# Twenty-nine matmuls that nobody reads, at the start of a planned two-layer transformer kernel

## The chip, the cores and the metric

The kernel runs on one core of a Trainium2 chip. A core has five engines with queues of their own: TensorE (PE, with its weight loads shown as PEld), VectorE (DVE), ScalarE (ACT), GpSimd (POOL) and SyncE (SP, which here only issues DMA transfers). Each engine works through its queue in order; semaphores hold an instruction until what it reads or overwrites is ready. The metric is the device time of one execution in microseconds (us). The kernel before takes 1548.72 us, the median of three runs (1548.48 to 1550.03).

## The reference

Two layers over 512 latent tokens and 256 context tokens of width 1024. What matters here is the opening of layer 0: a modulation vector from the conditioning, an RMS norm of the tokens, and the product with the QKV weights.

```python
silu_c = jax.nn.silu(c)
...
mod_lat = (silu_c @ ada_w[i] + ada_b[i])[:, None, :]
...
u_lat = modulate(rms_norm(h_lat, g_mix[i]), sh1, sc1)
u_ctx = modulate(rms_norm(h_ctx, g_mix[i]), csh1, csc1)
if i % N_MIXERS == 0:
    w = na_wqkv[j]
    ql, kl, vl = jnp.split((u_lat @ w).reshape(B, L, 3, H, dh), 3, axis=2)
    ...
    y_lat = neighborhood_attention(ql, kl, vl, kc, vc, na_rpb[j]) @ na_wo[j]
...
h_lat = h_lat + ga1 * y_lat
h_lat = h_lat + ga2 * squared_relu_mlp(
    modulate(rms_norm(h_lat, g_mlp[i]), sh2, sc2), mlp_w1[i], mlp_w2[i])
```

Attention adds a relative position bias to the scores (layer 0); layer 1 has sliding-window attention.

## The kernel before

The kernel holds its tokens transposed: feature tile f (0 to 7) has 128 features on the partitions and the tokens along the row. Every large product is made of three matmuls on values that are split into a high and a low part (`split`: ACT casts the high part, DVE or POOL subtracts it to get the low one).

The order of the work is not that of the source. `_build` records every operation as a step of a plan. `Plan.add` finds what each step depends on (also that a tile is read before it is overwritten), and `Plan.search` then sets the order on all engines. It goes through the program in pieces, ended by `mark()`, and for each tries many orders: a rank per step starts as the step's number, is changed by `hurry` where PE would stand still, and is shaken by random amounts that are drawn for groups of consecutive step numbers. The best order by its own table of costs is kept. Some operations have two possible engines (`gv`, `sv`, `squared`), and the search chooses between them. `build` issues all steps in that order at line 548, which is why nearly every row of the profile has this line.

The opening runs so:

- SP loads the constants (`cst`), the tokens (`xT`, four loads), and by the list `LOADS` the modulation weights of tile f (two halves `w01s[f, 0]` and `w01s[f, 1]`, by `load01`), the QKV weights of head pair 0 (`load0`), and the context tokens. `load` keeps these loads in their written order. Behind them come the QKV weights of pair 1 and the 32 transfers of `bias_tables`, which lay out the position bias in memory (`bias_i`, `bias_e`).
- `stats` squares each latent tile (ACT or DVE, four buffers) and sums it over the partitions with a matmul on the constant tile `ones`, into PSUM bank 4. ACT then makes the inverse root of it (two operations).
- `ada01(f)` makes the modulation sums of tile f: two groups of eight matmuls that are 32 columns wide, one per half of the weights. `mods01(f)` copies the sums to `row`, which is the first 128 columns of the second half's tile `w01s[f, 1]`, turns them with one small matmul on `pair`, and adds the bias on DVE. `mod0` then modulates tile f (DVE, ACT, DVE).
- `qkv0(0)` makes the QKV products of head pair 0 for six token tiles in banks 2 to 7, feature tile by feature tile as they come. A tile that is done goes through a head norm (ACT, DVE, POOL) and is transposed. `attn0(0)` follows: scores, and on DVE the position bias is added, which needs the bias loaded back from `bias_i` and `bias_e`. Products of pair 1 (256 columns) are put between.

Later pairs end in `attn0` with a multiplication by the inverse row sums, which DVE writes out and SP reads back through memory (`inv_d`), so that every partition has them.

Of the kernel before, what the change touches and what calls it, by code (L numbers as in the profile page):

```python
# [525 lines left out]
def build(nc, tc, a):  # L526

    with ExitStack() as es:
        plan, regions, cuts = _build(nc, tc, a, es)
        tiles, now, open_ = {}, -1, ExitStack()  # L530

        def real(x):
            return x.made(tiles) if isinstance(x, Late) else x

        def turn(k):

            open_.close()
            for j, (dtype, n) in enumerate(regions[k]):
                pool = open_.enter_context(tc.tile_pool(name=f"top{k}{j}", bufs=1))
                tiles[k, j] = pool.tile([128, n], dtype, name=f"R{k}{j}", tag="R")  # L540

        for step in plan.search(ROUNDS, TRIES, cuts):
            while step.epoch is not None and now < step.epoch:
                now += 1
                turn(now)
            for f, args, kw in step.calls:
                e = getattr(nc, NAMES[step.eng])
                tc.keep_in_program_order(getattr(e, f)(*map(real, args), **{k: real(x) for k, x in kw.items()}))  # L548
        open_.close()
# [16 lines left out]
def _build(nc, tc, a, es):  # L566
# [29 lines left out]
    @contextmanager  # L596
    def together():

        group.append(Step("PE"))
        yield  # L600
        plan.add(group.pop())

    v, s, g, pe, sy = (Engine(n) for n in ("vector", "scalar", "gpsimd", "tensor", "sync"))
# [3 lines left out]
    def squared(out, x):  # L607
        y = Step("ACT")
        y.forms = {"ACT": ("activation", (out, x, AF.Square), {}), "DVE": ("tensor_tensor", (), dict(out=out, in0=x, in1=x, op=ALU.mult))}
        y.calls, y.reads, y.writes = [y.forms["ACT"]], [x], [out]  # L610
        plan.add(y)
# [5 lines left out]
    def const(name, shape):  # L617
        return pool.tile(shape, F32, name=name, tag=name)
# [20 lines left out]
    banks = [psum.tile([128, 512], F32, name=f"pq{i}", tag=f"pq{i}")[:] for i in range(8)]  # L639

    class Banks:
# [3 lines left out]
        def next(self):  # L645
            self.i += 1
            return self.b[(self.i - 1) % len(self.b)]
# [14 lines left out]
    ones = const("ones", [128, 128])  # L662
# [38 lines left out]
    def load(out, in_):  # L701

        x = sy.dma_start(out, in_)
        if strict[0]:
            if strict[1:]:
                x.after = strict.pop().i
                x.deps.add(x.after)
            strict.append(x)
# [281 lines left out]
    def load0(p, units, eng=None):  # L990
        n = cols0(p)
        for q in units:
            r = (raw0 if p == 0 else raw).next(2 * n)
            load(r, a[f"wqkv0{min(p, 2)}"][max(0, p - 2), :, q * 2 * n : (q + 1) * 2 * n])
            u = (w00, w01, w0)[min(p, 2)].next()
            split(u[:, 0 : 2 * n], u[:, 2 * n : 4 * n], r, eng)
            for i in range(2):
                W0[p, 2 * q + i] = (u[:, i * n : (i + 1) * n], u[:, (2 + i) * n : (3 + i) * n])
# [388 lines left out]
    rows01, w01s = {}, {}  # L1387

    def load01(f):

        for i in range(2):
            w01s[f, i] = ada_ring.next()
            load(w01s[f, i], a["ada01"][f, :, 1024 * i : 1024 * i + 1024])

    def ada01(f):

        ps = banks[f % 2]
        for i in range(2):
            w = w01s[f, i].rearrange("p (k e n) -> p k e n", k=4, e=2)
            with together():  # L1400
                for k in range(0, 4, 2):
                    for e in range(2):
                        for j in range(2):
                            c = 32 * (2 * e + j)
                            pe.matmul(ps[c : c + 32, 0:128], s32[:, 4 * i + k + j, :], w[:, k + j, e], start=(4 * i + k == 0), stop=(4 * i + k == KT - 2), tile_position=(0, c))
        rows01[f] = w[:, 0, 0]
# [15 lines left out]
    def stats(h, R, sq, ps, summed):  # L1422

        st = Stats(R, R.shape[1], sq, ps)
        for f in range(KT):
            if not summed:
                st.step(h(f))
                continue
            q = sq.next()
            squared(q, h(f))  # L1430
            pe.matmul(ps[:, 0 : st.n], ones[:], q, start=f == 0, stop=f == KT - 1)
        st.finish(summed=summed)
# [8 lines left out]
    def more(n):  # L1441
        for _ in range(n):
            x = next(loads, None)
            if x is None:
                return
            if x == "c":
                load(hT_ctx, a["cT"])
            elif x == "w":
                load0(0, (w00.i,), g)
            else:  # L1450
                load01(x)

    more(5)
    stats(lambda f: hT_lat[:, f], Rb[:, 0:512], Ring(RX, 2048, 512, 4), banks[4], True)
    ada01(0)
    qk = qkv0(0)
    for f in range(KT):
        mods01(f)
# [33 lines left out]
    for p in range(7):  # L1492
        p_mm = Banks(2, 3, 4, 4, 4, 4) if p == 0 else Banks(4)
        at = (attn0(p), 14)
        if p < 4:
            n = (1, 3, 3, 3)[p]
# [609 lines left out]
    for gr in range(4):  # L2106
        seq = []
        n = 0
# [125 lines left out]
```

## Time and profile before

The profile is of one execution; times in it are counted from the span's start.

| | |
|---|---|
| that execution's own time | 1549.73 us |
| its span, first to last instruction | 1547.8 us |
| median of three runs | 1548.72 us |
| mean granted TensorE clock | 0.996 |
| TensorE busy | 1522.6 us |
| chain that ended last: share of PE, DVE, ACT | 92%, 4%, 2% |
| DMA, mean rate over the span | 119 GB/s |

An engine's busy time counts an instruction from start to end; on TensorE instructions overlap, and a multi-pass product of 32-bit values counts each pass. In a row of the time line stand the start, the length, the engine, the line, the operation, output and inputs, the count of merged instructions, and in brackets the idle time before with what ended it. The granted clock is the share of full speed that the TensorE clock was given.

### The profile page before, as it was taken

The numbers are of one execution on the slowest core, as the hardware profiler recorded it, in microseconds if no ns is written. First come the engines' busy times: TensorE is split into PE (matmuls) and PEld (weight loads), VectorE is DVE, ScalarE is ACT, GpSimd is POOL, SyncE is SP. The second block draws the span as 40 slices with busy tenths as digits, with TensorE's granted clock in tenths as the row PEclk, the third lists the DMA queues.
The fourth block names the chain that finished last, engine by engine and source line by source line (L and its number), as shares of the span: only waits on it lengthen the run. The fifth ranks groups of instructions, "written<-read, shape, count | busy, mean of one in ns | idle before, by whom it ended". The sixth has DMA issues, their size and how long they took to land.

```text
span 1547.8 us, 26105 instructions
## 1 busy us (share of the span) xinstructions
PE 1522.6 (98%) x9541; PEld 1350.7 (87%) x9541; DVE 1242.3 (80%) x2672; ACT 852.7 (55%) x1989; POOL 231.5 (15%) x223
## 2 busy tenths in 40 slices
PE   7999999999999999999999999999999999999999
PEld 4879888898899999999999998788778989898897
DVE  4888889867589998988888777899876897777764
ACT  4676666677466443344433454677784755555551
POOL 1110000101111322101111010321101312111110
PEclk9999999999999999999999999999999999999999
DMA  9654443215425433444444332001145343323321
GB/s 360 158 180 127 136 165 101 75 38 168 151 89 163 130 119 120 137 140 146 150 150 132 101 109 83 21 30 48 35 147 180 100 133 103 101 83 109 96 69 68
DMA packets 81473, 183.86 MB, mean 119 GB/s; under 512 B 9105, under 2 KB 26049, under 8 KB 81345
## 3 DMA queue, kind: packets, MB, share of 16 engines
q1 hardware_dynamic: 81344, 182.21, 37.0%
q8 instruction: 74, 1.21, 0.3%
q14 instruction: 55, 0.44, 0.1%
HBM read 172.64 MB, written 12.68 MB: 120 GB/s over the span
## 4 chain that ended last, share of the span: by engine, by line
PE 92%; DVE 4%; ACT 2%; DMA 1%; issue 1%; SPq 0%; POOL 0%; DVEq 0%; ACTq 0%; POOLq 0%
PE pq L548 92%; DVE FA L548 2%; DVE RA L548 1%; ACT FA L548 1%; DVE R L548 1%; ACT RA L548 0%; DMA R<-inv_d 0%; DMA FA<-bias_e 0%; DVE smalls L548 0%; ACT R L548 0%; DMA FA<-in_xT_dram 0%; SPq L548 0%; ACT smalls L548 0%; DVE mods L548 0%; POOL FA L548 0%
## 5 line engine op out<-in xcount | busy, mean ns | idle before, releaser
L548 PE MATMUL pq<-RA 128*128 128x256 f32 (+2 forms) x5906 | 1069.7, 335 | 7.8 <-DVE RA L548 4.5
L548 PEld LDWEIGHTS pq<-RA 128*128 128x128 f32 x5906 | 919.5, 190 | 95.4 <-issue 6.2
L548 PE MATMUL pq<-RA,R 128*128 128x256 f32 (+2 forms) x1896 | 339.3, 331 | 1.3 <-DVE FA L548 1.3
L548 ACT CAST RA<-FA 128x512 fp32r<-128x512 f32 (+4 forms) x390 | 232.3, 618 | 166.8 <-PE pq L548 123.3
L548 PEld LDWEIGHTS pq<-RA,R 128*128 128x128 f32 x1896 | 299.2, 189 | 26.1 <-DVE FA L548 2.1
L548 DVE TENSOR_TENSOR RA<-FA,RA 128x512 fp32r<-128x512 f32 (+4 forms) x350 | 256.0, 751 | 35.3 <-ACT RA L548 31.5
L548 DVE SCALAR_TENSOR_TENSOR FA<-pq,mods,FA 128x512 f32<-128x512 f32 (+1 forms) x323 | 201.1, 639 | 94.6 <-PE pq L548 92.6
L548 ACT ACTIVATE FA<-FA 128x256 f32<-128x256 f32 (+2 forms) x216 | 102.9, 484 | 60.0 <-DVE FA L548 48.4
L548 ACT CAST R<-FA 128x512 fp32r<-128x512 f32 x107 | 65.1, 619 | 106.0 <-PE pq L548 94.2
L548 PE MATMUL pq<-ident,FA 128*128 128x128 f32 x772 | 118.8, 275 | 4.4 <-issue 3.8
L548 POOL TENSOR_TENSOR RA<-FA,RA 128x512 fp32r<-128x512 f32 (+3 forms) x40 | 58.8, 1473 | 380.2 <-ACT RA L548 328.7
L548 ACT ACTIVATE FA<-FA,smalls 128x512 f32<-128x512 f32 (+1 forms) x120 | 88.7, 740 | 33.3 <-DVE smalls L548 32.5
L548 PEld LDWEIGHTS pq<-ident,FA 128*128 128x128 f32 x772 | 92.1, 141 | 16.6 <-issue 7.2
L548 DVE TENSOR_TENSOR FA<-FA 128x512 f32<-128x512 f32 (+3 forms) x163 | 88.7, 557 | 9.7 <-ACT FA L548 5.1
L548 ACT COPY R<-pq 128x512 f32<-128x512 f32 (+4 forms) x166 | 74.0, 469 | 34.8 <-PE pq L548 33.9
L548 ACT COPY FA<-pq 128x256 f32<-128x256 f32 (+5 forms) x114 | 44.3, 389 | 85.6 <-PE pq L548 82.7
L548 POOL TENSOR_TENSOR FA<-FA,smalls 128x256 f32<-128x256 f32 (+2 forms) x55 | 37.5, 681 | 294.5 <-DVE smalls L548 232.5
L548 DVE TENSOR_TENSOR R<-FA,R 128x512 fp32r<-128x512 f32 (+1 forms) x101 | 74.3, 743 | 8.6 <-ACT R L548 7.4
L548 ACT CAST RA<-R 128x256 fp32r<-128x256 f32 (+2 forms) x107 | 51.4, 489 | 51.2 <-PE pq L548 46.5
L548 DVE CUSTOM_DVE_ANT_0 R<-R,cst 128x512 bf16<-128x512 f32 (+1 forms) x64 | 78.5, 1226 | 0.1
L548 POOL TENSOR_TENSOR FA<-FA 128x256 f32<-128x256 f32 (+2 forms) x50 | 48.1, 970 | 188.0 <-ACT FA L548 85.9
L548 PE MATMUL pq<-R 128*64 128x256 f32 (+3 forms) x432 | 67.2, 450 | 0.7 <-DVE FA L548 0.7
(107 smaller groups left out, 1161.4 us busy)
## 6 DMA issues: line engine op xcount, KB each, us to landing
FA<-in_w_dram SPq DMA_DIRECT2D x128, 256.0 KB
FA<-in_w_dram SPq DMA_DIRECT2D x64, 512.0 KB
R<-in_ada_dram SPq DMA_DIRECT2D x54, 512.0 KB
FA<-in_ada_dram SPq DMA_DIRECT2D x26, 512.0 KB
FA<-in_wqkv_dram SPq DMA_DIRECT2D x24, 384.0 KB
FA<-in_ada_w_dram SPq DMA_DIRECT2D x16, 512.0 KB
FA<-in_wo_dram SPq DMA_DIRECT2D x16, 512.0 KB
FA<-in_wq_dram SPq DMA_DIRECT2D x8, 512.0 KB
```

The costliest lines, as they stand in the source:

```text
L548: tc.keep_in_program_order(getattr(e, f)(*map(real, args), **{k: real(x) for k, x in kw.items()}))
```

## The change

A helper `busy(n, x)` issues n matmuls of the constant tile `ones` with the first 128 columns of x, into bank 7, whose content nobody reads before the QKV products start it anew. Twenty-one of them, with `ones` as x, are written ahead of the norm sums; eight, with the second half of tile 0's modulation weights as x, behind the sums of tile 0.

```diff
+    def busy(n, x):
+        for _ in range(n):
+            pe.matmul(banks[7][:, 0:128], ones[:], x[:, 0:128], start=True, stop=True)
+
     more(5)
+    busy(21, ones)
     stats(lambda f: hT_lat[:, f], Rb[:, 0:512], Ring(RX, 2048, 512, 4), banks[4], True)
     ada01(0)
+    busy(8, w01s[0, 1])
     qk = qkv0(0)
```

The steps get other numbers, so the search draws other orders for the whole program. TensorE's queue opened so before (pq_66 to pq_73 are the PSUM banks 0 to 7, `s_82` is the silu of the conditioning, R the squares or the weights, FA and RA the large tiles):

```order
L548 MATMUL pq_70<-R_132,ones 128x512 x8
L548 MATMUL pq_66<-FA,s_82 32x128 x16
L548 MATMUL pq_67<-FA,s_82 32x128 x8
L548 MATMUL pq_66<-pair,FA 128x4
L548 MATMUL pq_67<-FA,s_82 32x128 x8
L548 MATMUL pq_66<-FA,s_82 32x128 x8
L548 MATMUL pq_68<-RA 128x512 x3
L548 MATMUL pq_69<-RA 128x512 x3
L548 MATMUL pq_70<-RA 128x512 x3
L548 MATMUL pq_71<-RA 128x512 x3
L548 MATMUL pq_67<-pair,FA 128x4
```

The same place in the changed kernel:

```order
L548 MATMUL pq_73<-ones 128x128 x21
L548 MATMUL pq_70<-R_143,ones 128x512 x7
L548 MATMUL pq_66<-FA,s_82 32x128 x8
L548 MATMUL pq_70<-R_143,ones 128x512
L548 MATMUL pq_66<-FA,s_82 32x128 x8
L548 MATMUL pq_73<-FA,ones 128x128 x8
L548 MATMUL pq_67<-FA,s_82 32x128 x8
L548 MATMUL pq_66<-pair,FA 128x4
L548 MATMUL pq_67<-FA,s_82 32x128 x8
L548 MATMUL pq_67<-pair,FA 128x4
L548 MATMUL pq_66<-FA,s_82 32x128 x8
L548 MATMUL pq_69<-RA 128x512
```

The 21 stand first, the 8 directly behind the modulation sums of tile 0, one group of those sums has moved ahead of the last norm sum, and the small product of tile 1 (`pq_67<-pair`) now stands ahead of the first QKV product and not behind twelve of them.

Further on in TensorE's queue, about the third and fourth feature tile, before:

```order
L548 MATMUL pq_71<-RA 128x512
L548 MATMUL pq_67<-R_132,s_82 32x128 x16
L548 MATMUL pq_68<-RA 128x512
L548 MATMUL pq_69<-RA 128x512
L548 MATMUL pq_70<-RA 128x512
L548 MATMUL pq_72<-FA,ones 128x256
L548 MATMUL pq_71<-RA 128x512
L548 MATMUL pq_67<-pair,R_132 128x4
L548 MATMUL pq_66<-R_132,s_82 32x128 x8
L548 MATMUL pq_66<-FA,s_82 32x128 x8
L548 MATMUL pq_67<-FA,s_82 32x128 x8
L548 MATMUL pq_66<-pair,FA 128x4
```

The same tiles now:

```order
L548 MATMUL pq_71<-RA 128x512
L548 MATMUL pq_67<-R_143,s_82 32x128 x8
L548 MATMUL pq_69<-RA 128x512
L548 MATMUL pq_67<-R_143,s_82 32x128 x8
L548 MATMUL pq_70<-RA 128x512
L548 MATMUL pq_68<-RA 128x512
L548 MATMUL pq_67<-pair,R_143 128x4
L548 MATMUL pq_68<-RA 128x512
L548 MATMUL pq_66<-R_143,s_82 32x128 x8
L548 MATMUL pq_72<-FA,ones 128x256
L548 MATMUL pq_69<-RA 128x512
L548 MATMUL pq_66<-FA,s_82 32x128 x8
```

The groups of modulation sums, which stood together, lie singly among the QKV products. From the first QKV product to the last `pair` product there were 4 visits to such groups, and there are 11 now. The last `pair` product of the opening stands behind 67 QKV products where it stood behind 93, and the first token tile has all its products after 99 of the 144 instead of 117. Over the whole program TensorE goes from products to transposes 252 times where it went 188 times.

SP's queue behind the bias tables, before (the last two table transfers, then the weights of pair 2 `wqkv02`, modulation weights `ada_w` and `ada0`, and the bias loaded back):

```order
L548 DMA bias_i_88<-in_rpb_i_dram 16x8x256
L548 DMA bias_e_89<-in_rpb_dram 16x8x128
L548 DMA FA_64<-in_wqkv02_dram 128x768 x2
L548 DMA FA_64<-in_ada_w_dram 128x1024 x2
L548 DMA FA_64<-in_ada0_dram 128x1024
L548 DMA FA_64<-bias_i_88 128x256 x2
L548 DMA FA_64<-bias_e_89 64x128 x4
```

Ahead of the tables and at their start, now:

```order
L548 DMA FA_64<-in_wqkv01_dram 128x512
L548 DMA FA_64<-in_ada_w_dram 128x1024
L548 DMA FA_64<-in_wqkv01_dram 128x512
L548 DMA bias_i_88<-in_rpb_i_dram 16x8x256
L548 DMA bias_e_89<-in_rpb_dram 16x8x128
L548 DMA FA_64<-in_wqkv01_dram 128x512
L548 DMA FA_64<-in_ada_w_dram 128x1024
L548 DMA FA_64<-in_ada0_dram 128x1024
L548 DMA FA_64<-in_wqkv01_dram 128x512
L548 DMA bias_i_88<-in_rpb_i_dram 16x8x256
```

The first two `ada_w` loads and the first `ada0` load, which stood between the tables and the bias loads, now stand ahead of 30 of the 32 table transfers; they write into the rows of the tokens that are modulated last. Behind the tables follow the two `wqkv02` loads and at once the bias. Ahead of the first score that needs the bias, TensorE's queue now has 14 more products of pair 1.

## The prediction

> **What bounds the kernel now.** I read the head of the page first, then the busy time of each engine by stretch, then the chain that ended last, then single rows of the time line.
>
> ```profile
> span 1547.8 us, 26105 instructions
> PE 1522.6 (98%) x9541; PEld 1350.7 (87%) x9541; DVE 1242.3 (80%) x2672; ACT 852.7 (55%) x1989; POOL 231.5 (15%) x223
> 0.00:5.70 5.70, 0.00 (x0) 0.00 (x0) 2.80 (x17) 2.13 (x3) 0.70 (x6) 1.00 0.64 197
> ...
> 15.30:17.50 2.20, 1.65 (x48) 1.11 (x48) 0.00 (x0) 2.13 (x3) 0.00 (x0) 1.00 1.04 425
> 17.50:20.90 3.40, 1.76 (x35) 1.24 (x36) 2.39 (x5) 1.15 (x4) 0.00 (x0) 1.00 1.07 364
> 20.90:24.30 3.40, 3.40 (x9) 2.39 (x10) 0.57 (x1) 0.77 (x3) 0.00 (x0) 0.50 1.04 402
> 24.30:27.50 3.20, 2.17 (x26) 1.62 (x24) 1.66 (x7) 1.31 (x4) 0.74 (x1) 0.99 1.03 408
> ...
> 76.40:82.60 6.20, 3.30 (x28) 1.66 (x27) 5.34 (x15) 3.63 (x12) 0.61 (x1) 0.98 0.84 259
> 82.60:86.00 3.40, 3.38 (x13) 2.91 (x14) 2.31 (x10) 2.80 (x7) 0.61 (x1) 0.53 0.97 370
> 86.00:980.00 894.00, 889.29 (x5349) 804.65 (x5348) 741.67 (x1548) 476.93 (x1108) 127.56 (x111) 1.00 0.39 123
> 980.00:987.00 7.00, 3.17 (x17) 2.43 (x16) 6.65 (x15) 1.77 (x6) 3.12 (x4) 0.99 0.13 37
> ```
>
> A row of the stretches gives its length, then busy time and instructions of PE, weight loads, DVE, ACT and POOL, the granted clock, and DMA share and GB/s. TensorE is the bound: 25.2 us of the span are without a matmul, and what PE loses it loses for good. The losses sit in few places: 5.70 at the start, 0.55 + 1.64 + 1.03 from 15.3 to 27.5, 2.90 ahead of the first attention scores, 4.71 in the 894 us behind, 3.83 at the layer boundary. Two of these stretches run at a granted clock of about 0.5, and ahead of each PE was busy only about half the time (1.76 of 3.40, 3.30 of 6.20).
>
> ```profile
> 15.34 0.70 ACT FA L548
> ...
> 16.59 1.04 ACT RA L548
> ...
> 20.74 4.78 PE pq L548 x14
> ...
> 76.29 5.31 DMA FA<-bias_e
> ```
>
> The chain has two serial pieces that this change touches. From the end of the norm sums (15.3) to the first real product (20.74) it goes through ACT and DVE. Ahead of 82 it goes through a bias load that SP's queue issues late.
>
> **The change part by part.** *Ahead: 21 matmuls.* Each is two passes of 128 columns. No row shows the form.
>
> ```profile
> 0.84 0.17 DVE L548 MEMSET ones<- 128x128 f32 x1 [0.84 <-PEq L2224]
> ...
> 6.72 0.34 PEld L548 LDWEIGHTS pq<-R,ones 128*128 128x128 f32 x1 [0.52 <-issue]
> ...
> 7.57 0.34 PEld L548 LDWEIGHTS pq<-R,ones 128*128 128x128 f32 x1 [0.52 <-issue]
> ...
> 11.47 0.63 ACT L548 ACTIVATE R<-FA 128x512 f32<-128x512 f32 x1 [1.30 <-DMA FA<-in_xT_dram]
> ...
> 13.42 0.19 PEld L548 LDWEIGHTS pq<-R,ones 128*128 128x128 f32 x1 [0.24 <-issue]
> 13.85 0.19 PEld L548 LDWEIGHTS pq<-R,ones 128*128 128x128 f32 x1 [0.24 <-issue]
> ...
> 16.05 0.63 ACT L548 ACTIVATE FA<-FA 128x512 f32<-128x512 f32 x1
> ...
> 215.06 1.36 PE L548 MATMUL pq<-ident,FA 128*128 128x128 f32 x11
> 216.18 5.35 PE L548 MATMUL pq<-RA 128*128 128x256 f32 x30
> ```
>
> A pass of the sums (same weights, 512 columns) starts every 0.85 us early and every 0.43 later: the array is at half speed at first, which the clock column does not show there. A quarter of the columns makes 0.21 and 0.11; eleven transposes of 128 columns, 0.10 each (215.06 to 216.18), say that the weight load hides. So 42 passes take 42 x 0.11 = 4.6 us at full and 42 x 0.21 = 8.8 at half speed; were each weight load of 0.34 exposed, 14.3. I take a mix, 3 us slow (14 passes) and 28 x 0.11, 6 us. They start when `ones` is there (1.0), end at about 7 (5.6 to 15.3 by the bounds), and delay the sums, whose first operand is there at 5.7. The sums cannot end before the last squares anyway, at 12.1 (row 11.47), since these wait for the last load. PE is then at full speed and has caught up: two operands (4 x 0.43) and the 32-wide group that now stands between them (0.46, below) are left, so the last pass ends at about 14.4, not 15.3: **-0.9 us**, which the chain passes on to the first product (19.8). At the upper bound it would be +7 at that point.
>
> *Behind: 8 matmuls.* 16 x 0.11 = 1.8 us (3.4 at half speed). They read the columns that ACT then overwrites with its copy of the modulation sums, so that copy waits for them. Their cover: between the last sum and that copy stand ACT's 0.70, the cast of 1.04 (both in the chain) and 0.63 (row 16.05), 2.37 us. Cost **0**; without the cover 1.8.
>
> *What they hold up: the clock.* The 17.5:20.9 stretch was at 1.76 of 3.40, and the next at 0.50. The 8 lie mostly ahead of it (14.9 to 16.7) and fill what stands there; what fills the stretch itself is the first products, from 19.8 instead of 20.74: 1.76 + 0.9 = 2.7 of 3.4. The half-speed stretch then goes: 3.40 x 0.5 = **-1.7**. (The other end is 0.) [...]
>
> *The new order.* The order is planned anew with 29 more steps, and every engine's queue differs. Three things in it I can price. First, the pair product of tile 1 now stands ahead of the products (the 1.03 us gap in 24.3:27.5 goes), but that of tile 2 comes after four to six products and waits for ACT's second modulated tile, some 0.7: **-0.3**. Second, 11 visits to the 32-wide groups lie among the products where there were 4.
>
> ```profile
> 27.49 4.83 PE L548 MATMUL pq<-RA 128*128 128x512 f32 x20 [0.65 <-ACT RA L548]
> ...
> 50.31 0.64 PE L548 MATMUL pq<-FA,s 128*32 128x128 f32 x16
> 50.77 1.06 PE L548 MATMUL pq<-R,s 128*32 128x128 f32 x32
> 51.65 0.62 PE L548 MATMUL pq<-FA,s 128*32 128x128 f32 x16
> 52.38 0.50 PE L548 MATMUL pq<-RA 128*128 128x512 f32 x1
> ...
> 53.40 0.28 PE L548 MATMUL pq<-pair,FA 128*128 128x4 f32 x2
> ...
> 55.99 2.20 DVE L548 SCALAR_TENSOR_TENSOR RA<-FA,mods,RA 128x512 fp32r<-128x512 f32 x4
> ```
>
> A group followed by another takes 0.46 (50.31 to 50.77), one followed by a product 0.73 (51.65 to 52.38): a turn costs 0.27, seven more **+1.9**. So the first layer's first products end -0.9 - 1.7 - 0.3 + 1.9 = **-1.0 us**.
>
> Third, SP's queue.
>
> ```profile
> 49.28 0.54 SPq L548 DMA_DIRECT2D bias_i<-in_rpb_i_dram  x1
> ...
> 71.28 1.76 SPq L548 DMA_DIRECT2D FA<-in_ada_w_dram  x2
> 73.14 0.38 SPq L548 DMA_DIRECT2D FA<-in_ada_dram  x1
> ...
> 75.54 2.72 SPq L548 DMA_DIRECT2D FA<-bias_e  x4
> ...
> 81.77 0.69 DVE L548 CUSTOM_DVE_ANT_1 FA<-pq,FA 128x512 f32<-128x512 f32 x1 [0.69 <-DMA FA<-bias_e]
> ...
> FA<-in_wqkv_dram SPq DMA_DIRECT2D x24, 384.0 KB
> ...
> FA<-in_ada_w_dram SPq DMA_DIRECT2D x16, 512.0 KB
> ```
>
> SP issues from 49.28 on, 0.6 us each, and the first bias add (81.77) waits for what it issues last. Two ada_w loads and one ada load move from behind the tables (71.28 to 73.52, 2.2 us of SP) to ahead of them. There they wait until the last modulated tile has been read, and hold the tables with them; before, DVE was done with it 4.8 us after the last pair product (53.40 to 58.2). That product now comes 26 products earlier in PE's order (26 x 0.24 = 6.2; 20 take 4.83 in row 27.49), and PE is 1.0 ahead: 46.2, and DVE done at 51. So the tables restart 1.7 later, the bias loads are issued 2.2 - 1.7 = 0.5 earlier, and behind two loads of 384 KB instead of these and three of 512 KB: 1.5 MB at some 400 GB/s (402 in 20.9:24.3) is 3.8 us less. I take 0.5 + 2.7 = 3.2 earlier, near 78.6 (bounds: 1.7 later, 4.3 earlier). The norm chain on DVE, which stands beside it, starts earlier too: the first tile ends 18 products sooner in the new order. PE comes to that wait 1.0 sooner but takes 14 more products of 256 columns with it (14 x 0.12 = 1.7): 2.9 + 1.0 - 3.2 - 1.7 is below nothing. I leave 0.9 of the 2.9 us standing, since the norm chain ends close by: **-2.0**. A wait that short leaves PE busy over 2.5 of 3.4 us, and the half-speed stretch of 82.6:86.0 goes with it: 3.40 x (1 - 0.53) = **-1.6**. Bounds for both: -4.5 and +1.
>
> *The rest.* From 86 on, PE had 4.7 + 3.8 us of gaps up to 987. The new order goes 64 more times from products to transposes and back; the groups before show nearly nothing for a turn (transposes keep 0.10): **+0.7** at 0.01 each. What gaps the new order has I cannot read from it: 0 +- 3.
>
> Sum: -1.0 - 2.0 - 1.6 + 0.7 = **-3.9 us**. The profiled execution took 1549.73 (1.9 outside its span): 1545.8. The median before, 1548.72, is 1.0 lower; from it, **1544.8 us**.
>
> **The rivals.** *Absorbed (0.27).* The wait before 82 stays where it is, since the tables restart over 4 us later than before behind the three moved loads, or the norm chain ends no sooner. For: DVE was busy 5.34 of 6.20 there. Against: fewer bytes ahead. Then only -1.0 + 0.7 is left, and the wait eats even that: 1548.4.
>
> *The clock falls anyway (0.13).* The matmuls on constants leave a stretch half empty by its place. [...] Against: 1.8 us of full matmuls in it. -3.9 + 1.7 = -2.2: 1546.5. [...]
>
> *Slower (0.13).*
>
> ```profile
> DVE FA L548 <- DMA R<-inv_d: 14.6, 3, 8.0
> ```
>
> DVE's multiply by the inverse row sums waits, in its place in DVE's queue, for a round trip through memory; three times before, the longest 8.0 us, with all later work of DVE behind it. The new order places all eight pairs' multiplies of each layer anew. If one is placed too early where the planned slack on PE is spent, PE stands too: 4.71 us of gaps in 894 say that today it rides over them. Price up to 8.0: -3.9 + 8.0 = +4.1, 1552.8. It decides the sign from 3.9 us of PE idle on.
>
> **How the numbers follow.** Forecast 0.47, its own range 1542.5 to 1547. About 0.2% (3.1 us) is what a measurement of this kernel can tell from no change. Below 1545.6 lie 0.38 of the forecast's chance and 0.06 of cases with a luckier rest: faster 0.44. Same: 0.09 of the forecast, the absorbed case and the clock case, less that 0.06: 0.43. Slower 0.13. The range takes in the absorbed case and part of the slow one: 1541 to 1551.
>
> **What would show it.** Right: the 16 passes of the sums 0.43 apart throughout; granted clock 1.00 in 20.9:24.3 and no half-speed stretch ahead of 100; the first product before 20; the first bias add near 78.6; PE gaps of about 5 us in 86:980. Wrong: the copy behind the 8 waiting for PE; passes of 0.3 us in the 21; the first bias add at 81 or later; DVE waiting for the inverse sums longer than 14.6 us in all.

## The result, and the profile after

The changed kernel takes **1553.07 us** (median of ten runs, 1551.43 to 1555.7); the kernel before, run beside it, 1548.6 (1545.97 to 1550.84). The ratio is 1.0032, with a 95% interval of 1.0023 to 1.004: it is slower, by 3.6 to 6.2 us. The forecast was 1544.8, the range ended at 1551. The profiled execution took 1554.57.

First the head of the page, then the stretches that the prediction speaks of, in the same order of columns (length, busy time of PE, weight loads, DVE, ACT, POOL, granted clock, DMA share, GB/s).

```profile
span 1552.8 us, 26177 instructions
PE 1534.2 (99%) x9599; PEld 1357.4 (87%) x9599; DVE 1249.7 (80%) x2680; ACT 850.5 (55%) x1986; POOL 210.9 (14%) x218
```

```profile
17.50:20.90 3.40, 3.10 (x49) 2.49 (x47) 2.00 (x4) 1.77 (x4) 0.00 (x0) 1.00 1.08 367
20.90:24.30 3.40, 3.24 (x40) 2.02 (x40) 2.14 (x6) 1.60 (x4) 0.00 (x0) 1.00 1.04 408
...
76.40:82.60 6.20, 5.43 (x42) 3.87 (x35) 5.75 (x19) 4.65 (x12) 0.61 (x1) 1.00 0.86 286
82.60:86.00 3.40, 3.40 (x31) 3.33 (x29) 3.38 (x12) 2.75 (x11) 0.59 (x1) 1.00 0.83 243
86.00:980.00 894.00, 886.74 (x5321) 801.71 (x5319) 744.77 (x1556) 476.34 (x1103) 114.77 (x105) 1.00 0.40 123
980.00:987.00 7.00, 6.27 (x19) 5.19 (x20) 4.51 (x11) 2.64 (x7) 0.73 (x1) 0.51 0.00 0
987.00:1235.00 248.00, 246.07 (x1720) 208.78 (x1719) 211.05 (x563) 172.46 (x428) 49.86 (x57) 1.00 0.25 80
1235.00:1253.00 18.00, 15.26 (x76) 12.59 (x75) 11.89 (x20) 6.19 (x13) 0.75 (x2) 0.81 0.57 177
1253.00:1540.00 287.00, 287.00 (x1773) 257.02 (x1773) 210.35 (x351) 144.32 (x313) 36.56 (x33) 1.00 0.30 91
```

Up to 86 us these figures are as forecast: the half-speed stretches at 20.9 and 82.6 are at 1.00, and PE is without work for 0.77 us of 76.4:82.6 where it was 2.90. The way there is another. The last of the opening's 144 QKV products starts at 66.29 us, where it started at 66.02: the opening gained nothing. And SP issues `bias_e` no sooner, at 75.54 as before. The rows around the wait, now:

```profile
75.54 2.42 SPq L548 DMA_DIRECT2D FA<-bias_e  x4
...
79.34 3.23 PE L548 MATMUL pq<-RA 128*128 128x256 f32 x18 [0.65 <-ACT FA L548]
...
80.49 0.69 DVE L548 CUSTOM_DVE_ANT_1 FA<-pq,FA 128x512 f32<-128x512 f32 x1 [0.35 <-DMA FA<-bias_e]
```

and the longest wait of PE there before, behind the bias add of 81.77:

```profile
82.62 2.05 PE L548 MATMUL pq<-RA 128*128 128x512 f32 x4 [1.28 <-DVE smalls L548]
```

The bias add that waits for its load comes 1.28 us sooner, and PE has eighteen products of pair 1 to do meanwhile.

What is new stands behind 980: 7 us at a clock of 0.51 (the kernel before has its half-speed stretch there from 986.9 on, for 3.4 us), and in 1235:1253 a loss of 2.74 us of PE and a clock of 0.81. To see where time was won and lost I counted both traces through matmul by matmul (products and transposes, each form with one price; the 29, the sums and the 32-wide groups left out) and noted when each had done the same amount:

| products done, us | before, at | after, at | difference |
|---|---|---|---|
| 50 | 89.98 | 85.62 | -4.4 |
| 850 | 951.29 | 945.89 | -5.4 |
| 925 | 1034.02 | 1031.67 | -2.3 |
| 1075 | 1222.68 | 1220.70 | -2.0 |
| 1100 | 1247.64 | 1251.78 | +4.1 |
| 1375 | 1525.75 | 1530.38 | +4.6 |

So the kernel gains 4.4 us ahead of 90 us, is 5.4 ahead at the layer boundary, loses 3.1 there and 6.1 in thirty microseconds around 1236. From row to row the difference moves by 1.0 or less elsewhere; within a row it can swing, since the two orders do the products of a stretch in another sequence (at 212 us it is near nothing, and at 320 it is some 4 again).

The time line at 1236 shows the loss (start, length, engine; the brackets give the idle time before and what ended it).

```profile
1220.50 16.28 SPq L548 DMA_DIRECT2D FA<-h_d  x8
...
1229.80 5.20 POOL L548 TENSOR_TENSOR RA<-FA,RA 128x256 fp32r<-128x256 f32 x1 [12.33 <-ACT RA L548]
...
1238.86 0.75 DVE L548 SCALAR_TENSOR_TENSOR FA<-pq,mods,FA 128x512 f32<-128x512 f32 x1 [2.75 <-DMA FA<-h_d]
...
1239.67 1.65 PE L548 MATMUL pq<-RA 128*128 128x512 f32 x3 [2.15 <-DVE FA L548]
1241.11 0.75 DVE L548 SCALAR_TENSOR_TENSOR FA<-pq,mods,FA 128x512 f32<-128x512 f32 x1 [1.49 <-DMA FA<-h_d]
...
1241.91 4.21 PE L548 MATMUL pq<-RA 128*128 128x512 f32 x9 [0.59 <-DVE FA L548]
```

And in the view of waits, for SP's queue between 1205 and 1262:

```profile
SPq L548 <- POOL RA L548: 5.2, 1, 5.2
```

One subtraction on POOL (the low part of a split, 128x256) takes 5.20 us, where the others like it take 0.74 to 1.53. It reads a tile that SP is about to fill again with the residual (`FA<-h_d`), so SP's queue waits 5.2 us for it; the residual lands late; DVE waits 2.75 and 1.49 us for it, and PE waits for DVE. Then the clock falls:

```profile
1236.00:1239.40 3.40, 1.52 (x13) 1.32 (x11) 0.65 (x2) 1.16 (x3) 0.00 (x0) 1.00 0.93 249
1239.40:1242.80 3.40, 2.54 (x5) 1.63 (x6) 1.91 (x4) 0.42 (x1) 0.00 (x0) 0.50 0.95 337
1242.80:1246.20 3.40, 3.40 (x10) 2.63 (x10) 1.72 (x4) 0.82 (x2) 0.00 (x0) 0.50 0.41 113
```

2.74 us of standing still (1.88 and 0.86) and two stretches at half speed with 5.94 us of matmuls in them (2.97 lost) make 5.7 of the 6.1. Before, the same place has no wait, although a subtraction on POOL is as slow there:

```profile
1222.63 10.64 SPq L548 DMA_DIRECT2D FA<-h_d  x8
...
1230.07 6.20 POOL L548 TENSOR_TENSOR RA<-R,RA 128x256 fp32r<-128x256 f32 x1 [2.06 <-ACT RA L548]
...
1235.59 1.40 DVE L548 SCALAR_TENSOR_TENSOR FA<-pq,mods,FA 128x512 f32<-128x512 f32 x2
```

That one reads R, which the residual does not fill, so SP does not wait for it and its 6.20 us cost nothing. What the new order lost is thus not the slow subtraction by itself, but that a load stands behind it.

### The profile page after: what moved, and what is told of

It is laid out like the page before. It is cut to its first block, busy times and chain, and to the rows that moved or that the text cites. A ratio compares the mean times of both kernels' runs of the same rounds, so it can differ in the third digit from the quotient of the medians.

```text
span 1552.8 us, 26177 instructions
## 1 busy us (share of the span) xinstructions
PE 1534.2 (99%) x9599; PEld 1357.4 (87%) x9599; DVE 1249.7 (80%) x2680; ACT 850.5 (55%) x1986; POOL 210.9 (14%) x218
## 4 chain that ended last, share of the span: by engine, by line
PE 94%; DVE 3%; DMA 2%; ACT 1%; issue 0%; SPq 0%; DVEq 0%; ACTq 0%
PE pq L548 94%; DVE FA L548 1%; DVE RA L548 1%; ACT RA L548 1%; ACT FA L548 1%; DMA RA<-silu_d 1%; DMA FA<-in_wqkv_dram 0%; DMA FA<-h_d 0%; DVE smalls L548 0%; DMA FA<-bias_e 0%; ACT R L548 0%; DVE R L548 0%; SPq L548 0%; ACT smalls L548 0%; DVEq L2236 0%
## 5 line engine op out<-in xcount | busy, mean ns | idle before, releaser
L548 PE MATMUL pq<-RA 128*128 128x256 f32 (+3 forms) x5906 | 1105.5, 336 | 6.4 <-DVE FA L548 2.9
L548 PE MATMUL pq<-RA,R 128*128 128x256 f32 (+2 forms) x1896 | 360.2, 331 | 0.3 <-DVE RA L548 0.3
L548 PEld LDWEIGHTS pq<-RA,R 128*128 128x128 f32 x1896 | 304.5, 189 | 25.5 <-DVE FA L548 0.6
L548 DVE TENSOR_TENSOR RA<-FA,RA 128x512 fp32r<-128x512 f32 (+4 forms) x351 | 260.1, 756 | 29.1 <-ACT RA L548 22.7
L548 ACT ACTIVATE FA<-FA 128x384 f32<-128x384 f32 (+2 forms) x218 | 104.0, 484 | 81.0 <-DVE FA L548 72.9
L548 PE MATMUL pq<-ident,FA 128*128 128x128 f32 x772 | 128.7, 276 | 5.8 <-DVE FA L548 3.6
L548 POOL TENSOR_TENSOR RA<-FA,RA 128x384 fp32r<-128x384 f32 (+2 forms) x39 | 58.2, 1493 | 441.7 <-ACT RA L548 395.8
L548 ACT COPY R<-pq 128x512 f32<-128x512 f32 (+4 forms) x173 | 78.6, 474 | 39.6 <-PE pq L548 37.8
L548 DVE TENSOR_TENSOR R<-FA,R 128x512 fp32r<-128x512 f32 (+1 forms) x116 | 85.7, 748 | 8.8 <-ACT R L548 7.1
L548 POOL TENSOR_TENSOR FA<-FA 128x256 f32<-128x256 f32 (+2 forms) x59 | 52.9, 907 | 223.7 <-ACT FA L548 87.1
```

## The experiments

All but the last four take the order of the steps from a list in place of the search, so that it can be put together from the two planned orders (`old`, `new`) or changed at one place:

```diff
-        for step in plan.search(ROUNDS, TRIES, cuts):
+        for step in given(plan):
```

Theory: the 29 matmuls are not what moved the time; the order that was planned with them is, and it gains in the first layer and loses at two places of the second. Rivals: the matmuls cost or gain by themselves; the loss is spread over the many turns between products and transposes, or over the waits for `inv_d`.

| run | order | the 29 | median, us | ratio to before, interval |
|---|---|---|---|---|
| changed kernel | new | all | 1553.07 | 1.0032 (1.0023 to 1.004) |
| e1 | old | all | 1547.64 | 0.9991 (0.9982 to 1.0) |
| e2 | new | none | 1553.91 | 1.0026 (1.0015 to 1.0036) |
| e3 | new, one POOL step on DVE | all | 1548.02 | 0.9986 (0.9977 to 0.9995) |
| e4 | new to step 8040, then old | all | 1543.66 | 0.9962 (0.995 to 0.9975) |
| e5 | as e4 | none | 1543.85 | 0.9963 (0.995 to 0.9975) |
| e6 | as e4, three SP loads back | all | 1549.51 | 0.9996 (0.9987 to 1.0005) |
| e7 | as e4 | the 21 | 1542.89 | 0.9959 (0.9947 to 0.9972) |
| e8 | as e4 | the 8 | 1543.23 | 0.9956 (0.9944 to 0.9969) |
| e9 | old to step 8040, then new | all | 1555.74 | 1.0037 (1.0023 to 1.0051) |
| e10 | new to step 9160, then old | all | 1544.94 | 0.9971 (0.9959 to 0.9982) |

Step 8040 is emitted at some 917 us, step 9160 at some 1040.

### The matmuls alone, and the new order without them (e1, e2)

```diff
 # e1: old order
+L548 MATMUL pq_73<-ones 128x128 x21
 L548 MATMUL pq_70<-R_132,ones 128x512 x8
 L548 MATMUL pq_66<-FA,s_82 32x128 x16
+L548 MATMUL pq_73<-FA,ones 128x128 x8
 # e2: new order
-L548 MATMUL pq_73<-ones 128x128 x21
-L548 MATMUL pq_73<-FA,ones 128x128 x8
```

> The order of before, step by step on every engine, with only the 29 matmuls put in (21 ahead of the first norm sum, 8 behind the modulation sums of tile 0). Theory (the matmuls gain at the start, the new order gives it back later): the norm sums end 0.9 us earlier and the half-speed stretch at 20.9 is gone (1.7 us), so 2.6 us below the 1548.6 us of before: about 1546.0 (1544 to 1549, the upper end if the wait ahead of 82 us takes it all). Rival 'the matmuls themselves cost': 1549 to 1553. Rival 'all of the loss is theirs': 1553.

> The new order on every engine, but the 29 matmuls left out. Theory: it loses what the matmuls gain in the opening and keeps the loss behind it, 1553.1 + 2.6 = 1555.7 us (1554 to 1557.5). Rival 'the matmuls themselves cost': below 1552. Rival 'they do nothing by themselves': 1553.

e1 came out at 0.9991, where the theory had 0.9983; e2 at 1.0026, level with the changed kernel's 1.0032 where 1.7 thousandths more were expected. By these two the matmuls are worth between nothing and 2.8 us in the old order, and nothing that can be told in the new one. My theory gave them 2.6 us: that lies at the edge of the interval in the old order, and it missed in the new one (1553.91, where 1554 to 1557.5 was expected). The opening of e2, without the 29 and with a half-speed stretch:

```profile
20.69 1.77 PE L548 MATMUL pq<-RA 128*128 128x512 f32 x4
...
24.60 5.30 PE L548 MATMUL pq<-RA 128*128 128x512 f32 x22
```

and of the changed kernel, with both:

```profile
1.09 7.85 PE L548 MATMUL pq<-ones 128*128 128x128 f32 x42 [1.09 <-DVE ones L548]
...
8.77 6.17 PE L548 MATMUL pq<-R,ones 128*128 128x512 f32 x14
...
16.62 0.69 ACT L548 ACTIVATE FA<-pq,eps 128x512 f32<-128x512 f32 x1 [4.43 <-PE pq L548]
17.08 2.05 PE L548 MATMUL pq<-FA,ones 128*128 128x128 f32 x16
...
19.17 0.27 ACT L548 COPY FA<-pq 128x128 f32<-128x128 f32 x1 [0.41 <-PE pq L548]
...
22.02 1.28 PE L548 MATMUL pq<-RA 128*128 128x512 f32 x4
...
24.62 3.65 PE L548 MATMUL pq<-RA 128*128 128x512 f32 x15
```

The first product comes 1.33 us later with the 29 (22.02 against 20.69), runs at full clock instead of half (1.00 against 0.53 in 20.9:24.3), and at the next long run of products both are level: 24.62 and 24.60. What the clock gives, the later norm sums (ACT starts at 16.62 against 15.95) and the longer chain behind them have taken. In e1 both half-speed stretches are gone too (1.00 in 20.9:24.3 and in 82.6:86.0), and the wait ahead of 82 is as long as before, since the bias add comes no sooner:

```profile
76.40:82.60 6.20, 3.29 (x26) 1.46 (x25) 5.05 (x15) 3.35 (x12) 0.42 (x1) 1.00 0.79 247
82.60:86.00 3.40, 3.31 (x22) 2.79 (x23) 3.27 (x13) 3.30 (x10) 0.61 (x1) 1.00 0.96 364
```

```profile
81.85 0.69 DVE L548 CUSTOM_DVE_ANT_1 FA<-pq,FA 128x512 f32<-128x512 f32 x1 [0.98 <-DMA FA<-bias_e]
```

### One step to another engine, and two orders joined (e3, e4)

```diff
 # e3: POOL's order, and DVE's
-L548 TENSOR_TENSOR RA<-FA,RA 128x256 x3
+L548 TENSOR_TENSOR RA<-FA,RA 128x256 x2
-L548 TENSOR_TENSOR RA<-FA,RA 128x256 x2
+L548 TENSOR_TENSOR RA<-FA,RA 128x256 x3
 # e4
-order = new
+order = new[:8040] + [x for x in old if x not in new[:8040]]
```

> The changed kernel with one subtraction (128x256, the one that took 5.20 us on POOL at 1229.80) done by DVE at its place in the order; nothing else differs. Theory: SP's reload of h_d waits for it no longer, DVE and PE stand 4 to 5 us less behind that load, and two half-speed windows of the clock (3.4 us lost) go or shrink to one: 1553.1 - 5 = 1548 us (1546.5 to 1549.5). Rival 'the loss is spread over many turns and the waits for inv_d': no change, 1553 (1552.5 to 1553.5).

> The changed kernel's order with the 29 matmuls for the first 8040 steps (up to the end of the first layer's MLP), and from there the order of before. Theory: it keeps the 5.4 us that the changed kernel is ahead by then and loses nothing at the layer boundary nor at 1230: 1548.6 - 5.4 = 1543.2 us (1541.5 to 1545). Rival 'being early there is worth nothing, the later waits take it': 1547 to 1549. [...]

Both came as the theory said: 1548.02 for 1548, and 1543.66 for 1543.2. One subtraction among 26,000 instructions is worth 5 us (5.9 against e2, which was run beside it). In e3 SP's reloads take 11.67 us instead of 16.28 and nobody waits for them:

```profile
1219.95 11.67 SPq L548 DMA_DIRECT2D FA<-h_d  x8
...
1235.49 1.40 DVE L548 SCALAR_TENSOR_TENSOR FA<-pq,mods,FA 128x512 f32<-128x512 f32 x2
```

The waits for `inv_d` are 12.6 us there and 14.7 in e4; in the changed kernel they are 16.7, the longest 7.5, and none of the two places of loss has one. e4 is faster than both kernels; by its ratio it is 5.9 us ahead of the kernel before.

### Is any of that the matmuls, and what carries the gain (e5 to e8)

```diff
 # e5: e4 without the 29; e7: without the 8; e8: without the 21
 # e6: e4, SP's order only, rows of table transfers cut
-L548 DMA FA<-in_ada_w_dram 128x1024
 L548 DMA FA<-in_wqkv_dram 128x512
 L548 DMA bias_i<-in_rpb_i_dram 16x8x256
...
-L548 DMA FA<-in_ada_w_dram 128x1024
-L548 DMA FA<-in_ada_dram 128x1024
...
 L548 DMA FA<-in_wqkv_dram 128x768 x2
+L548 DMA FA<-in_ada_w_dram 128x1024 x2
+L548 DMA FA<-in_ada_dram 128x1024
 L548 DMA FA<-bias_i 128x256 x2
```

> The kernel of the run with the new order up to step 8040 and the old behind it, without any of the 29 matmuls. Theory (the 29 bring the full clock in 20.9:24.3 and hand it back by holding the chain on ACT, so they are worth nothing together; all that is gained is the order of the first layer): 1543.7 us (1542.7 to 1544.7), first product at 20.7 at half clock instead of 22.0 at full. Rival 'they are worth the 1 to 2 us by which the run with the old order and the 29 came out lower': 1545 to 1546.

> The kernel with the new order up to step 8040 and the 29 matmuls; SP alone issues two ada_w loads and one ada load behind the bias tables again, as before. Theory (the moved loads are what ends the wait ahead of 82 us sooner): the first bias add that waits for its load comes at 82 instead of 80.5, PE stands some 2 us longer, a half-speed stretch may follow (1.6): 1543.7 + 2 to 3.6, about 1546.5 us (1545.5 to 1547.5). Rival 'it is the 14 more products and the earlier norm chain, not the loads': 1543.7 (within 0.7).

> The kernel with the new order up to step 8040, with the 21 matmuls and without the 8. Theory (the 21 delay the norm sums by 0.5 us, the 8 hold the clock): first product near 21.2, half clock in 20.9:24.3, so 0.5 us above the run without any: about 1544.2 us (1543.2 to 1545.2). Rival 'the 21 hold the clock by themselves': full clock there and about 0.8 us lower, 1542.9.

> The kernel with the new order up to step 8040, with the 8 matmuls and without the 21. Theory (the 8 hold the copy on ACT by 1.1 us and hold the clock): first product near 21.7, full clock in 20.9:24.3, about 1543.4 us (1542.4 to 1544.4). Rival 'without the 21 the clock falls all the same': about 1545.

e5 is at 0.9963 and e4 at 0.9962: with the order held, the 29 matmuls change nothing that can be measured (each interval reaches some 2 us to either side). e7 and e8 lie within the same interval. In their profiles either group alone leaves 20.9:24.3 at full clock (1.00), which is the rival's outcome for e7. From ACT's read of the norm sums to the first product it is 5.40 us with the 8 (changed kernel, e4, e8) and 4.74 without (e2, e7; 4.93 in e5, with its half-speed stretch from 19.17 on and 0.75 in 20.9:24.3), so the 8 hold the chain by some 0.66. The 21 do not run alike in every profile: their 42 passes take 7.85 us in the changed kernel, where they get closer at 7.21 us, from 0.21 to 0.11 us apart, and 7.66 in e1. ACT starts between 15.27 and 16.62 us in the runs with the new opening and the 21, and between 14.98 and 16.07 without them.

e6 gave back all: 1549.51, 3 us more than the theory's 1546.5, and by another path than the theory's. These loads feed a group of matmuls that stands ahead of the scores in PE's queue, and PE now waits for that load itself:

```profile
80.03 1.08 PE L548 MATMUL pq<-FA,s 128*32 128x256 f32 x8 [3.93 <-DMA FA<-in_ada_w_dram]
```

```profile
76.40:82.60 6.20, 2.39 (x17) 0.70 (x18) 2.87 (x7) 2.35 (x6) 0.61 (x1) 0.67 0.97 317
82.60:86.00 3.40, 3.40 (x16) 3.16 (x16) 1.87 (x7) 1.67 (x5) 0.00 (x0) 0.60 0.84 266
```

PE has 2.39 us of work in 6.20, and the granted clock is 0.67 there and 0.60 in the stretch behind. No bias add waits for its load in e6, and the tables start again at 52.87 us, with the three loads behind them, as at 52.93 in e4 with the three ahead: these loads did not hold the tables. So e6 shows that the new order of the products needs them early. It does not show that they bring the gain by an earlier bias; whether they would bring any in the old order of the products was not tried.

### The second half alone, and the boundary (e9, e10)

```diff
 # e9
+order = old_with_29[:8040] + [x for x in new if x not in old_with_29[:8040]]
 # e10
+order = new[:9160] + [x for x in old_with_29 if x not in new[:9160]]
```

> The reverse: the order of before with the 29 matmuls for the first 8040 steps, and from there the new order. Theory (from there on the new order is what costs: 3 us at the layer boundary, 6 us at 1230): 1547.6 of the old order with the 29, plus 9 to 10, about 1557 us (1554 to 1558; the lower end where no half-speed window follows the wait at 1236). Rival 'it loses only behind its own opening': 1548.

> The changed kernel's order up to step 9160 (about 1040 us, behind the layer boundary), then the order of before. Theory: the boundary costs 1.9 us more in the new order, the place at 1230 is the old one: 1543.7 + 1.9 = 1545.6 us (1544.8 to 1546.6). Rival 'nothing is lost at the boundary by the order': 1543.7. Rival 'the loss at 1230 comes with what stands ahead of it': 1550.

e9 takes 1555.74, 8.1 more than e1, which has the same order in the first layer: the second part of the new order costs this by itself. The subtraction takes 5.20 us again, from 1234.36, and the waits are back:

```profile
1234.36 5.20 POOL L548 TENSOR_TENSOR RA<-FA,RA 128x256 fp32r<-128x256 f32 x1 [12.34 <-ACT RA L548]
...
1243.51 0.75 DVE L548 SCALAR_TENSOR_TENSOR FA<-pq,mods,FA 128x512 f32<-128x512 f32 x1 [2.84 <-DMA FA<-h_d]
1244.32 0.98 PE L548 MATMUL pq<-RA 128*128 128x512 f32 x3 [2.23 <-DVE FA L548]
```

e10 comes at 1544.94, 1.3 above e4 (1.9 expected), and the intervals of the two overlap, so by times the boundary is not settled. By its trace the two waits of the changed kernel there (0.70 and 0.75) come with that part of the order:

```profile
1006.26 0.65 PE L548 MATMUL pq<-ident,FA 128*128 128x128 f32 x4 [0.72 <-DVE RA L548]
...
1008.98 2.96 PE L548 MATMUL pq<-RA 128*128 128x512 f32 x19 [0.75 <-ACT RA L548]
```

Counted through, e10 loses 1.9 us there, as the changed kernel does between 900 and 925 us of products. The rest of the 3.1 is a longer time at half clock behind 980, which e4 has with the old order too (0.50 in 979.7:983.1 and in 983.1:986.5) and e10 has not (0.72 and 0.78): it does not go with the order.

### Why does that subtraction take 5.20 us (m1 to m4)

```diff
-        plan, regions, cuts = _build(nc, tc, a, es)
...
+            keep(nc.scalar.copy(h[:, 256:512], x[:, 256:512]))
+            for k in range(1, n - 1):
+                dve(k, first, d[:, 768:1024], c)
...
+            keep(nc.gpsimd.tensor_tensor(out=g[:, 0:256], in0=x[:, 256:512], in1=h[:, 256:512].bitcast(F32), op=ALU.subtract))
```

> Leaves out the whole computation: the output is the input; only the disputed cost is measured. POOL does the subtraction (128x256, fp32r from f32 and fp32r) 12 to 13 times alone, beside 200 DVE subtractions of the same size from SBUF without a gap, beside 200 that read one operand from PSUM, beside ACT copies, and beside DVE subtractions with gaps. Theory (POOL gets its turn only in the gaps of DVE's run): 0.7 to 0.9 us alone, beside ACT and beside DVE with gaps under 2; 3 us and more beside the run without gaps. Rival 'the 5.2 us were a hiccup of that place': 0.7 to 1.3 everywhere.

> Leaves out the whole computation: the output is the input; only the disputed cost is measured. Now POOL's subtraction (128x256) becomes ready some 0.8 us after a run of DVE subtractions has begun: runs of 7, 13, 25, 7, 13, 25 operations from SBUF (some 2.4, 4.4 and 8.4 us), then 13 and 25 with one operand from PSUM, then 13 and 25 from SBUF with four POOL operations in a row. Theory (a POOL operation that comes into a run of DVE waits until the run has a gap, as at 1229.80, and in the run before it was the other way round because POOL was there first): it ends some 0.6 us behind the run, so about 2, 4 and 8 us long, also 0.9 or less where DVE reads PSUM. Rival 'the two take turns whoever is first': 0.9 to 1.3 us in every trial.

> Leaves out the whole computation: the output is the input; only the disputed cost is measured. As the run before, but every DVE operation writes a place of its own, so that none waits for an earlier one of DVE (in the run before each waited for the one two ahead). Trials: runs of 7, 13, 25 operations of 256 columns, 13 of 512 columns, 13 that write two places in turn (each waits, as in the run before), 13 that read PSUM, 13 of 256 again. Theory (DVE lets POOL in only where one of its operations has to wait; a run without waits holds POOL to its end, as at 1229.80): POOL takes about 2, 4 and 8 us in the first three, 8 in the fourth, 0.95 with the two places, 0.7 beside PSUM, 4 in the last. Rival 'turns in every case, so the 5.2 us need something else': 0.9 to 1.3 us in all.

> Leaves out the whole computation: the output is the input; only the disputed cost is measured. In both runs before, POOL's subtraction always became ready within 0.05 us of the start of a DVE operation; at 1229.80 it came 0.16 us into one. Here it comes at ten moments some 0.045 us apart, so over more than one DVE operation (0.34 us), each time into a run of 25 DVE subtractions of 256 columns, and then at five moments 0.09 us apart into runs of 13 of 512 columns. Theory (a request that falls inside a DVE operation is passed over until the run has a gap): 0.95 us for some of the moments, 7 us and more for others. Rival 'turns at every moment': 0.9 to 1.3 us in all fifteen.

(The lines are m2's: ACT's copy releases POOL's subtraction in the middle of a run of n DVE operations.) The theory fell in each of the four. POOL takes 0.72 us alone. Beside a run of DVE from SBUF it takes 0.89 to 0.96 (m2, m3), and the DVE operation that meets it 0.94 instead of 0.42; beside a run that reads PSUM, 0.72. Two trials of m2, one of each kind (a run of 25):

```profile
22.93 8.66 DVE L550 TENSOR_TENSOR c<-d 128x256 fp32r<-128x256 f32 x24
23.32 0.95 POOL L564 TENSOR_TENSOR g<-x,h 128x256 fp32r<-128x256 f32 x1 [4.86 <-ACT h L560]
...
57.44 8.03 DVE L550 TENSOR_TENSOR c<-p,d 128x256 fp32r<-128x256 f32 x24
57.81 0.72 POOL L564 TENSOR_TENSOR g<-x,h 128x256 fp32r<-128x256 f32 x1 [4.51 <-ACT h L560]
```

Operations of DVE with no waits among them (m3, 0.72 to 0.96 us) and fifteen moments of arrival, 0.045 us apart or more (m4, 0.72 to 1.21 us), brought no long one. In the changed kernel the same form, beside a run of DVE without a gap from 1229.30 to 1234.41, ended 0.59 us behind that run; in the kernel before, the subtraction of 6.20 us ended 0.60 behind the last DVE operation of its run that reads SBUF alone. Nine operations of DVE started while the one of 5.20 us stood.

The order does not decide it alone. The step that takes 6.20 us in the kernel before takes as long in e1, e4, e5 and e6, and 0.84 in e7, e8 and e10, with the same order on DVE and POOL around it:

```profile
1223.80 0.84 POOL L548 TENSOR_TENSOR RA<-R,RA 128x256 fp32r<-128x256 f32 x1 [2.05 <-ACT RA L548]
```

(e8). In all eight it starts 0.173 to 0.178 us into an operation of DVE, closer together than m4 could set it, so the moment of arrival is not ruled out. Why POOL takes so long there is **open**. The subtraction of the changed kernel takes 5.20 us in each of the three profiles that have it (changed, e2, e9). The ten times of the changed kernel (1551.43 and more) lie above all eleven of e3 (1549.78 and less), which speaks for the loss in each of them.

## Why the prediction was wrong, and where it was right

- *The 21* (end at about 7, sums end at 14.4, -0.9): wrong. They ended at 8.9 (42 passes in 7.85, 0.19 each): 27 passes at the slow pace where the forecast had 14. The sums then ran without a pause from 8.77 on, so that not the last squares but TensorE set their end. ACT could start at 16.62, over 2 us later than forecast and 1.3 later than before; how much of the 1.3 is these matmuls and how much the moment at which the passes got closer (7.21 us) is not separated.
- *The 8* (cost 0, hidden by 2.37 us of ACT): wrong. They ran from 17.08 to 19.1, the copy waited 0.41 for them, and the chain to the first product is 0.66 longer with them. First product: 22.02, forecast 19.8.
- *The clock* (-1.7): right. The stretch is at 1.00 in the changed kernel, e1, e3, e4 and e6 to e8, all with some of the 29, and not in the three kernels without (0.50 before, 0.53 in e2, 0.75 in e5). The stretch ahead of it had PE busy for 1.76 of 3.40 in the kernel before, and has 3.10 now; that the fuller stretch is what keeps the clock was my estimate, and at 82.6 the runs do not bear it out (last section). But the gain went into the late first product, and the two terms of -0.9 and -1.7 together came to nothing (24.62 against 24.60 in e2). With the turns to the 32-wide groups the opening was forecast at -1.0 and came to +0.3 (66.29 against 66.02); the price of a turn (+1.9 in all) was not measured apart.
- *SP's queue* (-2.0) *and the second half-speed stretch* (-1.6): right in size, wrong in the path. The tables restarted at 53.05, not 51, the loads of `bias_e` were issued at 75.54 as before, not 0.5 earlier, and the add that waits for them came at 80.49, not 78.6. PE's wait still shrank from 2.90 to 0.77, the 0.9 that was left standing: of the 2.90 only the 1.28 at 82.62 stood behind the bias add, and the new order has other products to do in that time. With the new first layer PE stands less there and the clock stays full (1.00 in 82.6:86.0) in the changed kernel, e2 to e5, e7 and e8, not in e6 (0.60); which of the moves in the order brings it is not shown. The sum to 86 us was forecast as -4.6 and measured as -4.4, which is in part luck, since the opening gave nothing and the stretch around the wait gave more.
- *The rest* (+0.7, and 0 +- 3): **this is the step that failed.** From there on it was -1.0 up to the boundary, and +10.0 behind it, against a band of 3: 6.1 around 1236, where one slow subtraction holds a reload (2.74 us of PE, and 2.97 by the half clock behind it), and 3.1 at the boundary. I said that the gaps of the new order cannot be read from it, and then gave them a band by the size of the old gaps. The forecast of -3.9 needed the second layer's order to be as good as the old one, which was a draw of a search.
- *The slower rival* had the sign and the kind (an engine waiting in its place for a transfer, with PE behind it). Its time of 1552.8 is near by luck: the wait left PE idle for 2.74 us, less than the 3.9 it asked for, and the half clock behind it, which it had not priced, made up the rest. It named the wrong transfer: `inv_d` waits went from 14.6 to 16.7 us, and neither place of loss has one. At 0.13 its chance was too low: there are many such places, and I priced one.
- *Absorbed* did not come about, since the wait shrank. In e1, with the old order, the wait is as long as before, but the opening had brought only 0.2 us that it could take (last QKV product at 65.80 against 66.02).

## What to carry to other kernels

Where a search plans the whole program, any edit draws a new order, and what is measured is that draw: hold the order and change the edit (e4 against e5), then hold the edit and change the order. An order can be joined from two draws at a place where both have done the same steps; here that is worth more (5.9 us) than the edit was ever forecast to bring. And a term for "everything else is replanned" needs a band taken from what single misplaced steps can cost, here 6 us, not from the idle time that is left in a well-planned order.

## What the runs showed of the hardware

- In m2 POOL's subtraction took 0.95 us, and the DVE subtraction with two SBUF inputs that met it 0.94, where they take 0.72 and 0.42 alone; beside DVE subtractions with a PSUM input it took 0.72. That nine operations of DVE start in the changed kernel while one of POOL stands (5.20 us), and that the same step takes 6.20 us in one profile and 0.84 in another, is shown by the kernels and not explained.
- Equal busy time ahead was not an equal clock: with PE busy for 3.30 of 6.20 us the kernel before fell to 0.53 in the next stretch, and e1, with 3.29, stayed at 1.00. The order did not decide it either: e9, whose order there is e1's, was busy for longer (3.94) and fell (0.64).

```profile
76.40:82.60 6.20, 3.94 (x27) 2.39 (x28) 5.28 (x17) 3.92 (x13) 0.00 (x0) 0.92 0.86 269
82.60:86.00 3.40, 3.40 (x19) 3.08 (x18) 2.46 (x9) 2.52 (x8) 0.61 (x1) 0.64 0.92 345
```

The half-speed stretches at 20.92, 82.36 and 986.89 us in the kernel before are 3.41 us long each, those at 979.99 and 1239.40 in the changed kernel 6.83. Over the 3.41 us directly ahead of the fall at 82.36 PE was busy for 0.43 of the time in the kernel before, and for 1.52 of 3.40 us ahead of the fall at 1239.40 in the changed kernel.
